# Hybrid encoder layer on one core: down stage begun during the last channel tile, its seven products reordered, its last product in groups of twelve, and two mixer orders changed

## The chip, the cores and the metric

The kernel runs on one core of a Trainium2 chip. The metric is the device time of one execution in microseconds (us), from three runs; the median is compared. A profile of one execution gives the trace that is read here.

The engines by the names of the trace: PE is the matrix engine (PEld its weight loads), DVE the vector engine, ACT the scalar engine, POOL the general engine, SP the engine that issues most transfers. Each works through its own instructions in order and waits on the others through semaphores. PEclk is the clock that was granted to PE, 1.00 being full speed.

## The reference, cut to what matters

One layer over 1280 tokens: 256 of a prompt (tiles t = 0, 1 of 128 tokens) and 1024 of a sample (t = 2 to 9), with shared weights, width 1024, feed-forward width 2816 = 22 tiles of 128 channels.

```python
h  = rmsnorm(x, g_pre_mix) * (1 + scale1) + shift1
y  = mixer(h)            # gated spatial mixing || gated linear attention, then @ w_out
x  = x + gate1 * rmsnorm(y, g_post_mix)
h  = rmsnorm(x, g_pre_ffn) * (1 + scale2) + shift2
up = conv(h @ w_up) + b_conv          # width-3 convolution along the tokens
gate, val = split(up)
y  = (silu(gate) * val) @ w_down      # 1280 x 2816 @ 2816 x 1024
x  = x + gate2 * rmsnorm(y, g_post_ffn)
```

Everything is fp32 to the outside. Inside, an fp32 operand is split into a rounded part `hi` and a rest `lo`, and a product is three matmuls: hi·hi, hi·lo, lo·hi.

## The kernel before, in words

**Stages.** Modulation vectors; in-projection; the mixer (spatial gating beside gated linear attention); `mix_out` (product with `w_out`, norm, residual); the up stage, first over the prompt (f = 0 to 21), then over the sample (f = 0 to 21); the down stage. PE's order is written out by hand; from the mixer on the other engines' instructions are put in order by a scheduler, from their dependences and estimated costs.

**Mixer.** For each pair of heads and chunk, `s3` adds into one PSUM bank: for each half j one full-height matmul `scT` (128x128) and two half-height matmuls against the state `St` (output 64 rows). There are 20 such steps, each among matmuls of the in-projection.

**mix_out.** Tile t loads the old x into the one buffer `xb` (L932, on SP's queue), squares y on ACT (L936), scales and adds it on DVE (L942, L944).

**Up stage of the sample.** A channel tile f is 7 products of 12 matmuls (84 at L1155) into three PSUM banks X, Y, V by a Strassen-Winograd scheme. `ug` and `uv` are taken out by ACT and DVE (L1162 to L1174), two convolutions follow (L1041, L1045), Silu (L1178), the product `av` on DVE (L1180), and a store of `av` to memory `g_d[f]`, 512 KB, on SP's queue (L1073). That store is kept in `gst` and issued a tile later, the last one behind the loop.

**Down stage.** `g` (tokens in two halves r, `half_tiles`) times `w_down` (columns in two halves n) is seven Strassen products, each 11 k-steps of two channel tiles (k = 0 to 10) x 5 token tiles j x 3 matmuls = 165 matmuls of 128x512 (L1300), in the order M3, M5, M2, M4, M1, M7, M6. Operand A is `g` (A00 of half r = 0 and even channel tiles, and so on; 320 KB each), B is `w_down` (256 KB each). For each k, `ops_of` loads what isn't resident (SP's queue), adds or subtracts on DVE where the product wants a sum (L1240, `saM`, `sbM`), and splits: hi on ACT (L91), lo on DVE (L92), into `aoM` (ring of 4) and `boM` (ring of 5). A00, A11 and B11 for k < 7 stay resident. Within a product PE runs k = 0, 1 together, then k = 2 to 8 one by one, and the last two k-steps (three in M6) j by j, so that a token tile ends early and `evac` adds its bank into the result y (L1280; or ACT where it is set). When a piece of y has had its last product, `finish` squares it on ACT (L1252) and multiplies it in place by the gate row G2 on DVE (L1253); when both halves of a row are done, `emit` loads x, makes the factor rf on POOL (L1261, L1262), and adds on DVE (L1265) and stores each half. M7 ends the five tiles of half 0, M6 those of half 1. The PSUM banks of the down stage are a pool of eight, opened when the up stage's pools are closed; G2 (1 MB) is loaded on ACT's queue.

Of the kernel before, what the change touches and what calls it, by code (L numbers as in the profile page):

```python
# [34 lines left out]
def encoder_kernel(ctx: ExitStack, tc: tile.TileContext, x_prompt, x_sample, c_prompt, c_sample,  # L35
# [693 lines left out]
    def s3(h, i):  # L729
# [9 lines left out]
        for j in range(2):  # L739
            nc.tensor.matmul(op[:, j, :], scT[n % RING][:, j, :], v[:, j, :], start=True, stop=False,  # L740
                             skip_group_check=True)
# [455 lines left out]
    nc.scalar.dma_start(Gbc2.rearrange("p s c -> p (s c)"), gate_d[1].to_broadcast([P, 2 * D]))
    ares, bres = {}, {}

    def load_a(r, c, k):  # L1200
        if r == c:
            if (r, k) not in ares:
                t = ares[(r, k)] = dr.tile([P, 640], F32, name=f"A{r}{c}_{k}")
                nc.sync.dma_start(t, g_d[2 * k + c][r])
# [4 lines left out]

    def load_b(c, n, k):  # L1210
        if c and n and k in bres:
            return bres[k]
# [5 lines left out]
        nc.sync.dma_start(raw, w_down[P * f:P * f + P, 512 * n:512 * n + 512])
# [9 lines left out]
    y = {}  # L1228
    ssq = {t: dn.tile([P, 2], F32, name=f"fssq{t}") for t in range(NT)}
    done = set()  # L1230

    def ops_of(i, k):
        name, a, b, _ = prods[i]
        src = []
        for what, terms, load, n, tag in ((0, a, load_a, 640, "sa"), (1, b, load_b, 512, "sb")):
            t0 = load(*terms[0], k)
            if len(terms) > 1:
                t1 = load(*terms[1], k)
                s = dr.tile([P, n], F32, tag=tag, name=f"{tag}{name}_{k}", bufs=2)
                nc.vector.tensor_tensor(out=s, in0=t0, in1=t1, op=ALU.add if terms[2] > 0 else ALU.subtract)  # L1240
# [16 lines left out]
    def emit(t, n):
# [5 lines left out]
        for n in range(2):  # L1263
            cs_ = slice(512 * n, 512 * n + 512)
            nc.vector.scalar_tensor_tensor(out=xo[:, cs_], in0=y[t][:, cs_], scalar=r, in1=xo[:, cs_],  # L1265
                                           op0=ALU.mult, op1=ALU.add)
# [24 lines left out]
    for i in range(len(prods)):  # L1291
        last = i == len(prods) - 1
        pss = [dp.tile([P, 512], F32, tag="d", name=f"dn{i}_{j}") for j in range(5)]
        ops = {}

        def mmk(j, k):
            ao, w = ops[k]
            cs_ = slice(P * j, P * j + P)
            for q, (ai, wi) in enumerate(((0, 0), (0, 1), (1, 0))):
                nc.tensor.matmul(pss[j], ao[:, ai, cs_], w[:, wi, :], start=(k == 0 and q == 0),  # L1300
                                 stop=(k == NK - 1 and q == 2))
# [51 lines left out]
```

## Time and profile before

| what | value |
|---|---|
| runs | 1463.11, 1468.05, 1467.68 us, median 1467.68 us |
| profiled execution | 1463.15 us, its span 1461.4 us |
| mean granted PE clock | 0.980 |
| PE busy | 1385.5 us, 95% of the span |
| DVE, ACT, POOL busy | 75%, 47%, 39% |
| down stage, 1155 matmuls | from 1177.58 us, last bank complete at about 1449.4 us |
| transfers | mean 144 GB/s; 277 and 307 GB/s in the two slices of about 37 us that follow 1169 us |

In the timeline a row is: start us, duration us, engine, line, operation, out<-in, shapes, count, and in brackets the idle time of that engine before it with what ended it. "SPq" and "ACTq" are transfers at the moment at which they are issued. In the windows a row gives the busy time and number of instructions of each engine in that stretch, then the granted PE clock, the share of the transfer engines and GB/s.

### The profile page before, as it was taken

The numbers are of one execution on the slowest core, as the hardware profiler recorded it, in microseconds if no ns is written. First come the engines' busy times: TensorE is split into PE (matmuls) and PEld (weight loads), VectorE is DVE, ScalarE is ACT, GpSimd is POOL, SyncE is SP. The second block draws the span as 40 slices with busy tenths as digits, with TensorE's granted clock in tenths as the row PEclk, the third lists the DMA queues.
The fourth block names the chain that finished last, engine by engine and source line by source line (L and its number), as shares of the span: only waits on it lengthen the run. The fifth ranks groups of instructions, "written<-read, shape, count | busy, mean of one in ns | idle before, by whom it ended". The sixth has DMA issues, their size and how long they took to land.

```text
span 1461.4 us, 20550 instructions
## 1 busy us (share of the span) xinstructions
PE 1385.5 (95%) x7057; PEld 1131.6 (77%) x7057; DVE 1089.4 (75%) x1653; ACT 692.5 (47%) x1405; POOL 576.3 (39%) x663
## 2 busy tenths in 40 slices
PE   8999989899997999898999999999999989999986
PEld 5886667677776888897978888888888868888875
DVE  5677667877744456798768888788778677879997
ACT  4544465645333234456654555545544345544342
POOL 3356756778763011443454444444444200001011
PEclk9999999999999999999999999999999999999998
DMA  9568542332223442565642222222222288551586
GB/s 300 195 226 289 189 124 84 117 97 63 84 91 110 145 152 101 154 175 156 196 131 85 87 76 66 83 87 87 87 87 80 81 277 307 181 169 65 186 287 207
DMA packets 204107, 210.53 MB, mean 144 GB/s; under 512 B 12968, under 2 KB 157668, under 8 KB 201700
## 3 DMA queue, kind: packets, MB, share of 16 engines
q1 hardware_dynamic: 199976, 200.10, 43.0%
q10 hardware_dynamic: 4028, 9.14, 1.6%
q8 instruction: 55, 0.90, 0.3%
q14 instruction: 48, 0.39, 0.1%
HBM read 171.16 MB, written 38.03 MB: 143 GB/s over the span
## 4 chain that ended last, share of the span: by engine, by line
PE 66%; DVE 10%; issue 7%; DMA 6%; POOL 6%; ACT 4%; SPq 0%; DVEq 0%; POOLq 0%; ACTq 0%
PE upX L1155 16%; PE dn L1300 15%; PE upV L1155 8%; PE ps_gb L338 5%; PE ps_ga L338 4%; PE upY L1155 4%; DMA raw_p<-in_w_up_dram 3%; PE y L878 3%; PE y L879 3%; PE y L881 2%; DVE St L723 1%; POOL macc L466 1%; DVE accP L1041 1%; POOL rstd L98 1%; PE ds L704 1%
## 5 line engine op out<-in xcount | busy, mean ns | idle before, releaser
L1300 PE MATMUL dn<-boM,aoM 128*128 128x512 f32 x1155 | 266.6, 393 | 11.1 <-ACT boM L91 5.9
L1300 PEld LDWEIGHTS dn<-boM,aoM 128*128 128x128 f32 x1155 | 219.4, 190 | 58.2 <-ACT boM L91 6.3
L92 POOL TENSOR_TENSOR ws_S<-S,ws_S 128x512 fp32r<-128x512 f32 x66 | 110.5, 1676 | 102.8 <-ACT ws_S L91 102.8
L1093 PE MATMUL upP<-hp,wp 128*128 128x256 f32 x1056 | 133.7, 287 | 14.4 <-DVE wp L92 12.9
L1093 PEld LDWEIGHTS upP<-hp,wp 128*128 128x128 f32 x1056 | 130.2, 192 | 17.6 <-DVE wp L92 15.4
L1155 PE MATMUL upX<-bop_T,ws_S 128*128 128x512 f32 x528 | 130.0, 395 | 2.8 <-ACT ug L1162 2.8
L92 POOL TENSOR_TENSOR ws<-raw_s,ws 128x512 fp32r<-128x512 f32 x44 | 77.2, 1756 | 120.6 <-ACT ws L91 120.6
L1155 PEld LDWEIGHTS upX<-bop_T,ws_S 128*128 128x128 f32 x528 | 100.0, 189 | 25.8 <-ACT ug L1162 3.3
L338 PE MATMUL ps_ga<-w_a,h1hi 128*128 128x512 f32 x320 | 105.6, 408 | 3.3 <-POOL w_a L92 2.6
L338 PE MATMUL ps_gb<-w_b,h1hi 128*128 128x512 f32 x320 | 105.9, 411 | 1.0 <-DVE w_b L92 0.5
L91 ACT ACTIVATE ws_S<-S 128x512 fp32r<-128x512 f32 x88 | 55.0, 628 | 85.6 <-DVE S L1135 53.8
L92 POOL TENSOR_TENSOR wp<-raw_p,wp 128x512 fp32r<-128x512 f32 x44 | 62.5, 1421 | 75.9 <-ACT wp L91 75.5
L1255 POOL TENSOR_SCALAR fssq<-fssq 128x1 f32<-128x1 f32 x10 | 9.7, 967 | 181.1 <-ACT junk L1252 181.1
L338 PEld LDWEIGHTS ps_ga<-w_a,h1hi 128*128 128x128 f32 x320 | 59.3, 190 | 22.5 <-issue 4.2
L91 ACT ACTIVATE aoM<-saM 128x640 fp32r<-128x640 f32 x55 | 40.6, 740 | 71.7 <-DVE saM L1240 27.4
L1135 DVE TENSOR_TENSOR S<-raw_s,raw_s 128x512 f32<-128x512 f32 x44 | 72.1, 1640 | 3.2 <-DMA raw_s<-in_w_up_dram 3.2
L338 PEld LDWEIGHTS ps_gb<-w_b,h1hi 128*128 128x128 f32 x320 | 57.8, 191 | 14.7 <-issue 2.4
L1041 DVE SCALAR_TENSOR_TENSOR ag<-ug,c,ag 128x1023 f32<-128x1023 f32 x44 | 56.5, 1284 | 15.9 <-ACT ag L1045 15.2
L91 ACT ACTIVATE wp<-raw_p 128x512 fp32r<-128x512 f32 x88 | 53.7, 627 | 30.8 <-DMA raw_p<-in_w_up_dram 25.4
L98 POOL TENSOR_TENSOR rstd<-ms,mhalf 128x2 f32<-128x2 f32 (+1 forms) x90 | 65.3, 726 | 7.3
L338 PE MATMUL ps_gb<-w_b,h1lo 128*128 128x512 f32 x160 | 65.3, 408 | 0.0
L338 PE MATMUL ps_ga<-w_a,h1lo 128*128 128x512 f32 x160 | 65.3, 408 | 0.0
(269 smaller groups left out, 3256.0 us busy)
## 6 DMA issues: line engine op xcount, KB each, us to landing
raw_d<-in_w_down_dram SPq DMA_DIRECT2D x104, 256.0 KB
raw_p<-in_w_up_dram SPq DMA_DIRECT2D x88, 256.0 KB
raw_s<-in_w_up_dram SPq DMA_DIRECT2D x88, 256.0 KB
A<-g_d SPq DMA_DIRECT2D x66, 320.0 KB
wa<-in_w_ada_dram SPq DMA_DIRECT2D x16, 1024.0 KB
g_d<-av SPq DMA_DIRECT2D x22, 512.0 KB
wa<-in_w_ada_dram SPq DMA_DIRECT2D x16, 512.0 KB
vr_d<-vr SPq DMA_DIRECT2D x20, 256.0 KB
```

What stands on the lines that cost most here:

```text
L91: nc.scalar.activation(w[:, 0, :], raw, AF.Copy)
L92: (eng or nc.gpsimd).tensor_tensor(out=w[:, 1, :], in0=raw, in1=w[:, 0, :].bitcast(F32), op=ALU.subtract)
L98: nc.gpsimd.tensor_tensor(out=r, in0=ms, in1=mhalf.to_broadcast([P, n]) if n > 1 else mhalf, op=ALU.pow)
L338: nc.tensor.matmul(ps, st, mv, start=(i == 0), stop=(i == n - 1))
L878: nc.tensor.matmul(ys[n], mh[:, kt, :], wos[(kt, n)][:, 0, :], start=(i == 0), stop=False)
L879: nc.tensor.matmul(ys[n], mh[:, kt, :], wos[(kt, n)][:, 1, :], start=False, stop=False)
L881: nc.tensor.matmul(ys[n], ml[:, kt, :], wos[(kt, n)][:, 0, :], start=False, stop=(i == KT - 1))
L1041: nc.vector.scalar_tensor_tensor(out=acc[:, o:o + b - a], in0=src[:, a:b], scalar=c2[:, i, fi:fi + 1], in1=acc[:, o:o + b - a], op0=ALU.mu ...
L1093: nc.tensor.matmul(ps[:, half, :], st, hp[:, hi, kt, :], start=(kt == 0 and i == 0 and half == 0), stop=(kt == KT - 1 and i == 2), skip_gr ...
L1135: nc.vector.tensor_tensor(out=s, in0=a, in1=b, op=op)
L1155: nc.tensor.matmul(ps, w[:, wi, P * j:P * j + P], bops[(b, j)][:, hi, :], start=(start and j == 0 and i == 0), stop=(stop and j == 3 and i ...
L1300: nc.tensor.matmul(pss[j], ao[:, ai, cs_], w[:, wi, :], start=(k == 0 and q == 0), stop=(k == NK - 1 and q == 2))
```

## The change

1. **Down stage begun earlier.** In f = 21 the operands of M3 for k = 0, 1 go into a pool of their own, `er`: A00 (`ea_k`) and the two weight tiles (`raw_e`) are loaded at the head of the last channel tile, their difference is made in place, and they are split (`eao`, `ebo`). The 30 matmuls of k = 0, 1 stand directly behind the last matmul of the up stage. To have banks for it, the down stage takes its PSUM tiles from the up stage's two pools (`bank`) and opens none. Since A00_0, A00_1, B11_0 and B11_1 did not become resident in M3, M5 loads them.
2. **Buffers given out in a set order** (`new_as`, `firsts` and the loops behind it), so that the addresses of these tiles follow the order of these calls.
3. **Order of products** M3, M5, M1, M7, M4, M2, M6: M4 now ends the tiles of half 0, and in M4 the piece (1, 0) is set, in M2 added to.
4. **`finish` writes into a tile of its own** (`yg`, ring of 2) for the second half of a row.
5. **Tail of four k-steps** in M6: twelve matmuls for each j in place of nine.
6. **`s3`**: both scT matmuls first, then the four St matmuls; the bank is started once.
7. **`mix_out`**: `xb` is loaded on ACT's queue.

```diff
-            nc.tensor.matmul(op[:, j, :], scT[n % RING][:, j, :], v[:, j, :], start=True, stop=False,
+            nc.tensor.matmul(op[:, j, :], scT[n % RING][:, j, :], v[:, j, :], start=(j == 0), stop=False,
                              skip_group_check=True)
+        for j in range(2):
             for e in range(2):
...
-        xloads[t] = nc.sync.dma_start(xt, x_rows(t))
+        xloads[t] = nc.scalar.dma_start(xt, x_rows(t))
...
+    def early_load():
+        for k in range(2):
+            a = er.tile([P, 640], F32, name=f"ea_{k}")
+            nc.sync.dma_start(a, g_d[2 * k][0])
+            b = [raw_tile(f"raw_e{k}_{c}") for c in range(2)]
+            for c in range(2):
+                nc.sync.dma_start(b[c], w_down[P * (2 * k + c):P * (2 * k + c) + P, 512:1024])
+            eops.append((a, b))
+
+    def early_split():
+        for k, (a, b) in enumerate(eops):
+            nc.vector.tensor_tensor(out=b[0], in0=b[0], in1=b[1], op=ALU.subtract)
+            ao = er.tile([P, 2, 640], F32R, name=f"eao_{k}")
+            bo_ = er.tile([P, 2, 512], F32R, name=f"ebo_{k}")
+            split(ao, a, nc.vector)
+            split(bo_, b[0], nc.vector)
+            eops[k] = [[t[:, h, :] for h in range(2)] for t in (ao, bo_)]
+
+    def bank(name):
+        i = banks["i"] % 8
+        banks["i"] += 1
+        return gpa.tile([P, 512], F32, tag="g", name=name) if i in (3, 4) else fp.tile([P, 512], F32, tag="f", name=name)
...
+        if f == NFF - 1:
+            er, er_close = pool("er", side="right")
+            early_load()
         while gst:
             gst.pop(0)()
...
         nc.scalar.activation(uv[:, lo], X, AF.Copy)
+        if f == NFF - 1:
+            early_split()
+            pss0 = [bank(f"dn0_{j}") for j in range(5)]
+            for k in range(2):
+                for j in range(5):
+                    mmk(pss0[j], *eops[k], j, k)
...
     gst.pop(0)()
     sf_close()
     hb_close()
+    er_close()
...
-    dp, dp_close = pool("dp", bufs=8, space=PSUM)
...
+    firsts = [new_as("A_first"), new_sum("sa", 640, "sa_first")]
+    for k in range(2):
+        new_ar(1, k)
+    firsts += [new_sum("sb", 512, "sb_first"), new_ao("ao_first"), new_bo("bo_first")]
+    for k in range(2, NK):
+        new_ar(1, k)
...
-             ("M2", ((1, 0), (1, 1), 1), ((0, 0),), ((1, 0, "set"), (1, 1, "sub"))),
-             ("M4", ((1, 1),), ((1, 0), (0, 0), -1), ((0, 0, "add"), (1, 0, "add"))),
              ("M1", ((0, 0), (1, 1), 1), ((0, 0), (1, 1), 1), ((0, 0, "add"), (1, 1, "add"))),
              ("M7", ((0, 1), (1, 1), -1), ((1, 0), (1, 1), 1), ((0, 0, "add"),)),
+             ("M4", ((1, 1),), ((1, 0), (0, 0), -1), ((0, 0, "add"), (1, 0, "set"))),
+             ("M2", ((1, 0), (1, 1), 1), ((0, 0),), ((1, 0, "add"), (1, 1, "sub"))),
              ("M6", ((1, 0), (0, 0), -1), ((0, 0), (0, 1), 1), ((1, 1, "add"),)))
...
-        nc.vector.tensor_tensor(out=y[t][:, cs_], in0=y[t][:, cs_], in1=Gbc2[:, 0 if t < 2 else 1, cs_], op=ALU.mult)
+        yg = y[t][:, cs_] if (t, 1 - n) not in done else dn.tile([P, 512], F32, tag="yg", name=f"yg{t}", bufs=2)
+        ygs[(t, n)] = yg
+        nc.vector.tensor_tensor(out=yg, in0=y[t][:, cs_], in1=Gbc2[:, 0 if t < 2 else 1, cs_], op=ALU.mult)
...
-        pss = [dp.tile([P, 512], F32, tag="d", name=f"dn{i}_{j}") for j in range(5)]
+        pss = [bank(f"dn{i}_{j}") for j in range(5)] if i else pss0
...
-        tail = 3 if last else 2
-        for k in range(NK - tail):
+        tail = 4 if last else 2
+        for k in range(0 if i else 2, NK - tail):
```

The order of the transfers that SP issues where the two stages meet, before (`raw_d01_k` and `B11_k` are the weight tiles of M3, `A00_k` its operand A, `g_d20` and `g_d21` the stores of the last two channel tiles):

```order
L1073 DMA g_d20_85<-av20_10947 128x2x512
L1204 DMA A00_0_11134<-g_d0_65 128x640
L1218 DMA B11_0_11138<-in_w_down_dram 128x512
L1204 DMA A00_1_11148<-g_d2_67 128x640
L1218 DMA B11_1_11152<-in_w_down_dram 128x512
L1204 DMA A00_2_11192<-g_d4_69 128x640
L1218 DMA B11_2_11196<-in_w_down_dram 128x512
L1204 DMA A00_3_11221<-g_d6_71 128x640
L1073 DMA g_d21_86<-av21_11091 128x2x512
L1218 DMA B11_3_11225<-in_w_down_dram 128x512
```

And now:

```order
L1279 DMA raw_d01_2_11224<-in_w_down_dram 128x512
L1279 DMA raw_d01_3_11251<-in_w_down_dram 128x512
L1279 DMA raw_d01_4_11278<-in_w_down_dram 128x512
L1279 DMA raw_d01_5_11305<-in_w_down_dram 128x512
L1074 DMA g_d20_85<-av20_10947 128x2x512
L1074 DMA g_d21_86<-av21_11155 128x2x512
L1264 DMA A00_2_11211<-g_d4_69 128x640
L1279 DMA B11_2_11212<-in_w_down_dram 128x512
L1264 DMA A00_3_11209<-g_d6_71 128x640
L1279 DMA B11_3_11210<-in_w_down_dram 128x512
```

The loads of A00 and B11 for k = 2 and A00 for k = 3 stood ahead of the last store; now they stand behind it, and four weight tiles stand ahead of both stores.

DVE where the up stage ends, before (`av21` is the last product of the up stage, `sbM3_k` the difference of two weight tiles of M3 for k, `aoM3_k` and `boM3_k` the lo parts):

```order
L1041 SCALAR_TENSOR_TENSOR av21_11091<-uv21_10998,c2_5056,av21_11091 128x1023 x2
L1240 TENSOR_TENSOR sbM3_0_11140<-raw_d01_0_11136,B11_0_11138 128x512
L1180 TENSOR_TENSOR av21_11091<-ag21_11090,av21_11091 128x1024
L92 TENSOR_TENSOR aoM3_0_11142<-A00_0_11134,aoM3_0_11142 128x640
L92 TENSOR_TENSOR boM3_0_11145<-sbM3_0_11140,boM3_0_11145 128x512
L1240 TENSOR_TENSOR sbM3_1_11154<-raw_d01_1_11150,B11_1_11152 128x512
```

And now:

```order
L1042 SCALAR_TENSOR_TENSOR av21_11155<-uv21_11013,c2_5056,av21_11155 128x1023 x2
L1224 TENSOR_TENSOR av21_11155<-ag21_11154,av21_11155 128x1024
L1301 TENSOR_TENSOR sbM3_2_11227<-raw_d01_2_11224,B11_2_11212 128x512
L1301 TENSOR_TENSOR sbM3_3_11254<-raw_d01_3_11251,B11_3_11210 128x512
L92 TENSOR_TENSOR aoM3_2_11229<-A00_2_11211,aoM3_2_11229 128x640
L92 TENSOR_TENSOR boM3_2_11232<-sbM3_2_11227,boM3_2_11232 128x512
```

The first work of DVE for the down stage at this place is that of k = 2, and the difference for k = 3 stands ahead of both lo parts of k = 2.

DVE in the tail of M6, before:

```order
L1280 TENSOR_TENSOR y1_11431<-dn6_0_13174,y1_11431 128x512
L1253 TENSOR_TENSOR y1_11431<-y1_11431,G2_11117 128x512
L1265 SCALAR_TENSOR_TENSOR xo1_13488<-y1_11431,rf1_13490,xo1_13488 128x512 x2
L1280 TENSOR_TENSOR y6_11441<-dn6_1_13175,y6_11441 128x512
L1280 TENSOR_TENSOR y7_11451<-dn6_2_13176,y7_11451 128x512
L1253 TENSOR_TENSOR y6_11441<-y6_11441,G2_11117 128x512
L1265 SCALAR_TENSOR_TENSOR xo6_13510<-y6_11441,rf6_13512,xo6_13510 128x512 x2
```

And now:

```order
L1343 TENSOR_TENSOR y1_11448<-dn6_0_13189,y1_11448 128x512
L1316 TENSOR_TENSOR yg1_13490<-y1_11448,G2_11177 128x512
L1328 SCALAR_TENSOR_TENSOR xo1_13492<-y1_11448,rf1_13494,xo1_13492 128x512
L1328 SCALAR_TENSOR_TENSOR xo1_13492<-yg1_13490,rf1_13494,xo1_13492 128x512
L1343 TENSOR_TENSOR y6_11458<-dn6_1_13190,y6_11458 128x512
L1316 TENSOR_TENSOR yg6_13516<-y6_11458,G2_11177 128x512
L1328 SCALAR_TENSOR_TENSOR xo6_13518<-y6_11458,rf6_13520,xo6_13518 128x512
```

Before, the additions of the second and third tile stood together, and of the fourth and fifth; now each tile's additions, product and sums stand together before the next tile's begin.

More of the change, by code (lines that the diff above doesn't have):

```diff
@@ L1116, in encoder_kernel, with mmk @@
     sf, sf_close = pool("sf")
+    NK = NFF // 2
+    er = None
+    eops = []
+    def early_load():
[14 more added lines that the diff above has]
+            eops[k] = [[t[:, h, :] for h in range(2)] for t in (ao, bo_)]
+    banks = {"i": 0}
+    def bank(name):
+        i = banks["i"] % 8
+        banks["i"] += 1
+        return gpa.tile([P, 512], F32, tag="g", name=name) if i in (3, 4) else fp.tile([P, 512], F32, tag="f", name=name)
+    def mmk(ps, ao, w, j, k):
+        cs_ = slice(P * j, P * j + P)
+        for q, (ai, wi) in enumerate(((0, 0), (0, 1), (1, 0))):
+            nc.tensor.matmul(ps, ao[ai][:, cs_], w[wi], start=(k == 0 and q == 0), stop=(k == NK - 1 and q == 2))
     for f in range(NFF):
@@ L1198, in encoder_kernel @@
     ares, bres = {}, {}
+    new_as = lambda name: dr.tile([P, 640], F32, tag="as", name=name, bufs=4)
+    new_sum = lambda tag, n, name: dr.tile([P, n], F32, tag=tag, name=name, bufs=2)
+    new_ao = lambda name: dr.tile([P, 2, 640], F32R, tag="ao", name=name, bufs=4)
+    new_bo = lambda name: dr.tile([P, 2, 512], F32R, tag="bo", name=name, bufs=5)
+    new_ar = lambda r, k: ares.setdefault((r, k), dr.tile([P, 640], F32, name=f"A{r}{r}_{k}"))
+    new_br = lambda k: bres.setdefault(k, dr.tile([P, 512], F32, name=f"B11_{k}"))
+    firsts = [new_as("A_first"), new_sum("sa", 640, "sa_first")]
[4 more added lines that the diff above has]
+        new_ar(1, k)
+    for k in (1, 0):
+        new_ar(0, k), new_br(k)
+    for k in range(NK - 1, 1, -1):
+        new_ar(0, k)
+        if k < 7:
+            new_br(k)
+    loaded = set()
     def load_a(r, c, k):
         if r == c:
-            if (r, k) not in ares:
-                t = ares[(r, k)] = dr.tile([P, 640], F32, name=f"A{r}{c}_{k}")
-                nc.sync.dma_start(t, g_d[2 * k + c][r])
+            if (r, k) not in loaded:
+                loaded.add((r, k))
+                nc.sync.dma_start(ares[(r, k)], g_d[2 * k + c][r])
             return ares[(r, k)]
-        t = dr.tile([P, 640], F32, tag="as", name=f"A{r}{c}_{k}", bufs=4)
+        t = new_as(f"A{r}{c}_{k}")
         nc.sync.dma_start(t, g_d[2 * k + c][r])
@@ L1210, in load_b @@
     def load_b(c, n, k):
-        if c and n and k in bres:
+        if c and n and ("b", k) in loaded:
             return bres[k]
@@ L1214, in load_b @@
         if c and n and k < 7:
-            raw = bres[k] = dr.tile([P, 512], F32, name=f"B11_{k}")
+            raw = bres[k]
+            loaded.add(("b", k))
         else:
@@ L1222, in encoder_kernel @@
              ("M5", ((0, 0), (0, 1), 1), ((1, 1),), ((0, 1, "add"), (0, 0, "neg"))),
[L1223 to L1224 removed]
              ("M1", ((0, 0), (1, 1), 1), ((0, 0), (1, 1), 1), ((0, 0, "add"), (1, 1, "add"))),
              ("M7", ((0, 1), (1, 1), -1), ((1, 0), (1, 1), 1), ((0, 0, "add"),)),
+             ("M4", ((1, 1),), ((1, 0), (0, 0), -1), ((0, 0, "add"), (1, 0, "set"))),
+             ("M2", ((1, 0), (1, 1), 1), ((0, 0),), ((1, 0, "add"), (1, 1, "sub"))),
              ("M6", ((1, 0), (0, 0), -1), ((0, 0), (0, 1), 1), ((1, 1, "add"),)))
[L1228 removed]
+    y, ygs = {}, {}
     ssq = {t: dn.tile([P, 2], F32, name=f"fssq{t}") for t in range(NT)}
@@ L1238, in ops_of @@
                 t1 = load(*terms[1], k)
-                s = dr.tile([P, n], F32, tag=tag, name=f"{tag}{name}_{k}", bufs=2)
+                s = new_sum(tag, n, f"{tag}{name}_{k}")
                 nc.vector.tensor_tensor(out=s, in0=t0, in1=t1, op=ALU.add if terms[2] > 0 else ALU.subtract)
@@ L1242, in ops_of @@
             src.append(t0)
-        ao = dr.tile([P, 2, 640], F32R, tag="ao", name=f"ao{name}_{k}", bufs=4)
+        ao = new_ao(f"ao{name}_{k}")
         split(ao, src[0], nc.vector)
-        wo_ = dr.tile([P, 2, 512], F32R, tag="bo", name=f"bo{name}_{k}", bufs=5)
+        wo_ = new_bo(f"bo{name}_{k}")
         split(wo_, src[1], nc.vector)
-        return ao, wo_
+        return [[t[:, h, :] for h in range(2)] for t in (ao, wo_)]
     def finish(t, n):
@@ L1264, in emit @@
             cs_ = slice(512 * n, 512 * n + 512)
-            nc.vector.scalar_tensor_tensor(out=xo[:, cs_], in0=y[t][:, cs_], scalar=r, in1=xo[:, cs_],
+            nc.vector.scalar_tensor_tensor(out=xo[:, cs_], in0=ygs[(t, n)], scalar=r, in1=xo[:, cs_],
                                            op0=ALU.mult, op1=ALU.add)
@@ L1292, in encoder_kernel @@
         last = i == len(prods) - 1
-        pss = [dp.tile([P, 512], F32, tag="d", name=f"dn{i}_{j}") for j in range(5)]
+        pss = [bank(f"dn{i}_{j}") for j in range(5)] if i else pss0
         ops = {}
[L1296 to L1301, printed above, removed]
-        tail = 3 if last else 2
-        for k in range(NK - tail):
+        tail = 4 if last else 2
+        for k in range(0 if i else 2, NK - tail):
             ops[k] = ops_of(i, k)
-            if k == 0:
+            if i and k == 0:
                 continue
-            if k == 1:
+            if i and k == 1:
                 for js in ((0, 1, 2), (3, 4)):
@@ L1311, in encoder_kernel @@
                         for j in js:
-                            mmk(j, kk)
+                            mmk(pss[j], *ops[kk], j, kk)
                 continue
             for j in range(5):
-                mmk(j, k)
+                mmk(pss[j], *ops[k], j, k)
         for k in range(NK - tail, NK):
@@ L1319, in encoder_kernel @@
             for k in range(NK - tail, NK):
-                mmk(j, k)
+                mmk(pss[j], *ops[k], j, k)
             evac(i, j, pss[j])
-    for close in (dp_close, dn_close, dr_close, rp_close, cp_close, dram_close):
+    for close in (fp_close, gpa_close, dn_close, dr_close, rp_close, cp_close, dram_close):
         close()
```

3 lines of the change are left out of this document (removed).

## The prediction

> **What bounds the kernel now.** I read the page first (who is busy, the chain that ended last), then PE's waits, then the places of these waits in the timeline, and there the granted clock.
>
> ```profile
> PE 1385.5 (95%) x7057; PEld 1131.6 (77%) x7057; DVE 1089.4 (75%) x1653; ACT 692.5 (47%) x1405; POOL 576.3 (39%) x663
> ...
> GB/s 300 195 226 289 189 124 84 117 97 63 84 91 110 145 152 101 154 175 156 196 131 85 87 76 66 83 87 87 87 87 80 81 277 307 181 169 65 186 287 207
> ...
> PE 66%; DVE 10%; issue 7%; DMA 6%; POOL 6%; ACT 4%; SPq 0%; DVEq 0%; POOLq 0%; ACTq 0%
> ```
>
> PE is the bound. The change removes no matmul, so it can only win at PE's waits, at matmuls that run on a lower clock, and in the tail behind PE's last matmul. PE's waits of the stages that are touched:
>
> ```profile
> PE pt_m L781 <- DMA m<-m_d: 7.3, 1, 7.3
> PE dn L1300 <- ACT boM L91: 5.9, 1, 5.9
> ...
> PE dn L1300 <- DVE aoM L92: 4.2, 1, 4.2
> ```
>
> The first is at the head of the product with w_out, the second where the up stage meets the down stage (the join), the third inside M6. The timeline at the join:
>
> ```profile
> 1166.11 2.88 PE L1155 MATMUL upV<-bop,ws_S 128*128 128x512 f32 x12
> ...
> 1168.83 2.88 PE L1155 MATMUL upX<-bop_T,ws 128*128 128x512 f32 x12
> ...
> 1173.73 1.06 ACT L1178 ACTIVATE ag<-ag 128x1024 f32<-128x1024 f32 x1
> ...
> 1176.78 1.22 DVE L1180 TENSOR_TENSOR av<-ag,av 128x1024 f32<-128x1024 f32 x1
> ...
> 1177.58 0.79 PE L1300 MATMUL dn<-boM,aoM 128*128 128x512 f32 x1 [5.86 <-ACT boM L91]
> ...
> 1178.02 0.37 SPq L1073 DMA_DIRECT2D g_d<-av  x1
> 1178.44 0.47 SPq L1218 DMA_DIRECT2D B<-in_w_down_dram  x1
> ...
> 1178.65 0.69 DVE L92 TENSOR_TENSOR boM<-sbM,boM 128x512 fp32r<-128x512 f32 x1
> ...
> 1179.39 10.79 PE L1300 MATMUL dn<-boM,aoM 128*128 128x512 f32 x40 [1.02 <-DVE boM L92]
> ...
> 1179.85 0.82 DVE L92 TENSOR_TENSOR aoM<-A,aoM 128x640 fp32r<-128x640 f32 x1
> ...
> 1179.97 0.33 ACTq L1197 DMA_DIRECT2D G<-gate_d  x1
> 1180.32 0.43 SPq L1218 DMA_DIRECT2D B<-in_w_down_dram  x1
> ...
> 1180.85 0.38 SPq L1204 DMA_DIRECT2D A<-g_d  x1
> ...
> 1188.56 0.69 DVE L1240 TENSOR_TENSOR sbM<-raw_d,B 128x512 f32<-128x512 f32 x1 [3.36 <-DMA B<-in_w_down_dram]
> ...
> 1189.80 0.74 ACT L91 ACTIVATE aoM<-A 128x640 fp32r<-128x640 f32 x1 [2.65 <-DMA A<-g_d]
> ```
>
> Twelve matmuls at full clock start 1168.83 - 1166.11 = 2.72 us apart, 0.2267 each; the last of the up stage ends at 1177.58 - 5.86 = 1171.72. The last product of the up stage on DVE ends at 1178.0, and only then does SP issue its store. Later loads take long here: the weight tile for k = 4, issued at 1180.32, is used 8.24 us later after a wait for it, the A tile issued at 1180.85 after 8.95 us. The clock and the transfers in windows of 1 us, at the join and at M6:
>
> ```profile
> 1175.00:1176.00 1.00, 0.00 (x0) 0.00 (x0) 1.00 (x1) 1.00 (x2) 0.00 (x0) 0.85 0.00 0
> ...
> 1181.00:1182.00 1.00, 1.00 (x4) 0.81 (x3) 1.00 (x3) 0.27 (x2) 0.00 (x0) 0.50 0.99 306
> 1182.00:1183.00 1.00, 1.00 (x5) 0.73 (x5) 1.00 (x2) 0.59 (x1) 0.00 (x0) 0.74 0.86 252
> ...
> 1414.00:1415.00 1.00, 0.00 (x0) 0.00 (x0) 0.72 (x2) 0.00 (x0) 0.00 (x0) 0.81 0.70 262
> ...
> 1421.00:1422.00 1.00, 1.00 (x5) 0.81 (x4) 1.00 (x2) 0.42 (x1) 0.00 (x0) 0.77 0.91 308
> ```
>
> 0.85 in one window means that the clock halved at 1175.70, 4.0 us after PE stopped; 0.74 that it was whole again at 1182.5. At M6 it halved at 1414.6 and was whole at 1421.5. Matmuls lose half of the time in between. Full transfer engines move about 306 GB/s. The stall in M6:
>
> ```profile
> 1401.24 0.68 DVE L1280 TENSOR_TENSOR y<-dn,y 128x512 f32<-128x512 f32 x1
> ...
> 1404.19 1.42 DVE L1265 SCALAR_TENSOR_TENSOR xo<-y,rf,xo 128x512 f32<-128x512 f32 x2 [0.46 <-POOL rf L1262]
> ...
> 1410.37 1.42 DVE L1265 SCALAR_TENSOR_TENSOR xo<-y,rf,xo 128x512 f32<-128x512 f32 x2 [0.44 <-POOL rf L1262]
> ...
> 1414.60 1.42 DVE L1265 SCALAR_TENSOR_TENSOR xo<-y,rf,xo 128x512 f32<-128x512 f32 x2 [0.28 <-DMA xo<-x_d]
> 1415.93 0.82 DVE L92 TENSOR_TENSOR aoM<-saM,aoM 128x640 fp32r<-128x640 f32 x1
> ...
> 1416.80 3.78 PE L1300 MATMUL dn<-boM,aoM 128*128 128x512 f32 x8 [4.23 <-DVE aoM L92]
> ```
>
> From 1401.24 to 1415.93 DVE does nothing but end the five tiles of half 0, and the lo part that PE needs for k = 2 stands behind that. The stall costs 4.23 us and half of 1416.80 to 1421.5, 2.3 us.
>
> **The change part by part.** The sum starts from the profiled execution, 1463.15 us (span 1461.4), which is 4.5 us under the median of the runs.
>
> Join. Before, PE lost 5.86 + 1.02 us in waits, and between 1177.58 and 1182.5 it worked 3.9 us at half clock, which is 2.0: 8.9 in all. Now the 30 matmuls of k = 0, 1 follow the up stage directly, 30 x 0.2267 = 6.8 us, and end at 1178.5. That part I take as done: their sums and splits stand in f = 20 and before, where DVE and ACT aren't what PE waits for, at most one difference of DVE, 0.69 us, late, and this moves nothing if k = 2 decides. But k = 2 now decides. Its loads (A00 and B11) stand on SP behind the last store, which waits for DVE until 1178.0. So they are issued from about 1178.4, one each 0.43 us: A00_2, B11_2, A00_3, B11_3 at about 1179.8. DVE takes the difference for k = 3 ahead of the lo parts of k = 2, so B11_3 counts too. Store and four loads are 512 + 640 + 512 KB = 1.70 MB; from 1178.9 at 306 GB/s that is 5.6 us, 1184.5. G2's 1 MB is now issued right behind Silu (ends at 1174.8), near 1175.5, into idle transfer engines (0.00 above), and I take it as out of the way. Then 0.69 + 0.82 + 0.69 on DVE (the rows of 1188.56, 1179.85, 1178.65): k = 2 starts at 1186.7. PE's idle time is 8.2 us, with some 2.0 at half clock behind it (1.6 to 2.3): 10.2, so the join is +1.3. Low end: the four loads alone, 3.8 us from 1178.5, k = 2 at 1184.6, -1.1. High end: B11_3 lands 8.95 us after its issue, at 1188.8, k = 2 at 1191.0, 12.5 + 2.3, +6.0. What the edit takes from PE's wait for k = 0, 1 it gives back at k = 2.
>
> Order of products. M4 now does what M7 did, and M2 waits where M6 did: five additions, five products with G2 and ten sums stand between M4's last matmul and the lo part of k = 2. Two things are lighter: M4 and M2 need one sum for each k and not two, so DVE isn't late at the start of the burst (0.7 us or so: M7's first tile was complete 24 + 30 matmuls, 12.2 us, before the stall of 1412.6, at about 1400.4), and `yg` lets the product go ahead without ACT, with other work in front of the sums, which can save up to the 0.46 + 0.44 + 0.28 us of waits. That leaves 2.3 to 4.2; I take 2.7, -1.5. The clock fell 2.0 us after PE stopped in M6, 4.0 us at the join; a stall of 2.7 lies between, so I take half of the 2.3 us away: -1.2. Doubt about the burst itself takes 0.7 back: -2. Ends: all of it gone, -6.5; nothing gained and M4 half a microsecond worse, +0.5.
>
> [...]
>
> The tail:
>
> ```profile
> 1437.66 11.72 PE L1300 MATMUL dn<-boM,aoM 128*128 128x512 f32 x51
> ...
> 1441.26 0.69 DVE L1280 TENSOR_TENSOR y<-dn,y 128x512 f32<-128x512 f32 x1 [2.19 <-PE dn L1300]
> ...
> 1444.15 1.41 DVE L1265 SCALAR_TENSOR_TENSOR xo<-y,rf,xo 128x512 f32<-128x512 f32 x2 [0.72 <-POOL rf L1262]
> ...
> 1445.48 1.28 DVE L1280 TENSOR_TENSOR y<-dn,y 128x512 f32<-128x512 f32 x2
> ...
> 1456.55 1.41 DVE L1265 SCALAR_TENSOR_TENSOR xo<-y,rf,xo 128x512 f32<-128x512 f32 x2
> ```
>
> PE ends at T = 1449.38, DVE at 1457.96, T + 8.6. One tile alone takes 1445.48 - 1441.26 = 4.22 us on DVE, most of it waiting for ACT and POOL; before, tiles two to five went in pairs, 6.2 us each. Now the first tile is complete four groups of 12 before T, T - 10.9 (before T - 8.2), but DVE does the tiles one after the other: -10.9 + 0.2 + 5 x 4.22 = T + 10.4, +1.8 us. Ends: -2.4, if ACT and POOL are quicker than in that row since the product no longer waits; +2.5. With four k-steps in the tail all four `aoM` tiles are in use, and the last can be split only when k = 6 is through: ACT 0.74, DVE 0.82 + 0.69 against nine matmuls, 2.0 us: +0.2.
>
> The mixer. Where a half-height matmul is followed by a full one, the weight load stands 0.17 us without cause:
>
> ```profile
> 268.20 0.30 PEld L740 LDWEIGHTS o<-v,scT 128*128 128x128 f32 x2 [0.17 <-issue]
> ...
>   issue: 3.4, 20
> ```
>
> One of two such places goes in each of 20 steps, 3.4 us at most; some groups wait for other engines later and swallow it: -2 (-3.4 to 0).
>
> `xb` on ACT's queue. Ten issues move from SP to ACT. SP gains nothing where PE waits. The first one now stands ahead of the load behind PE's 7.3 us wait:
>
> ```profile
> 471.35 0.38 SPq L773 DMA_DIRECT2D m<-m_d  x1
> ```
>
> 512 KB at 306 GB/s are 1.7 us, if all of it is in the way: +0.5 (0 to +1.7).
>
> M5's four reloads are 1.15 MB. They lie beside 37 us of matmuls; the transfers of this time (307 and 181 GB/s in the page's slices from 1205 and 1242) also hold what is fetched ahead, so 0; without that cover 1.15 MB / 306 GB/s = 3.8 us.
>
> Sum: +1.3 - 2 + 1.8 + 0.2 - 2 + 0.5 = -0.2, so 1463.0 on the profiled execution's level and 1467.5 on the median's. The runs lie at both, so I say 1465.
>
> **The rivals.** Faster, by M2: the burst on DVE fits beside PE's 30 matmuls of k = 0, 1, so the whole stall and its half clock go (-6.5); with the lighter loads at the join (-1.1) and all of the mixer's 3.4, against +2.5 in tail and transfers, -8.5: 1456.5. For it: the waits of 1.2 us within the burst and the late start of 0.7. Against it: these make 1.9, and the stall is 4.2.
>
> Faster, by the join: the loads of k = 2 aren't late after all, and the 8.9 us go but for 1 or so: 1465 - 9 = 1456. Against it stands SP's order.
>
> Slower, by the join: everything that is issued between 1175.5 and 1182 shares the transfer engines: store, G2 and eight loads, 512 + 1024 + 2304 KB = 3.93 MB, 12.8 us at 306 GB/s from 1178.9. B11_3 then lands at 1191.7, k = 2 starts at 1193.9: PE loses 15.4 + 2.3, +8.8 in place of +1.3: 1472.5. For it: the tiles that took 8.24 and 8.95 us. Against it: G2 was issued among those, at 1179.97, and comes earlier now. It decides (over 0.5% against the median) once k = 2 starts after 1194.
>
> [...]
>
> **How the numbers follow.** 0.5%, about 7.3 us, is what a measurement of this kernel can tell from no change. Forecast (terms cancel) 0.57, M2 free 0.25, join free 0.07, join late 0.11. The two faster rivals end near that bound, so some of them is "same", as some of the forecast's lower part is "faster": faster 0.31, same 0.59, slower 0.10. The range reaches to the rivals on both sides: the forecast alone gives 1458 to 1470, with them 1454 to 1473.
>
> **What would show it.** Join: down matmuls directly behind the up stage, then one wait of about 8 us at x30, with DVE waiting for a B tile; a wait under 3 us proves me wrong there. M2: a wait of 2 to 4 us for aoM at k = 2, with or without half clock; none at M6. Tail: DVE ends 10 us behind PE, not 8.6. Mixer: L740's idle time of 3.4 us at issue about gone, the in-projection's end some 2 us earlier. pt_m's wait within 1.7 us of 7.3. The forecast is wrong if a new wait shows in M5 or M1, or if k = 2 at the join starts before 1183 or after 1194.

## The result, and the profile after

The changed kernel takes 1475.19 us (median of 11 runs), the kernel before 1467.68 us in the same comparison: ratio 1.0057, 95% interval 1.0043 to 1.0071. It is slower by some 8 us, more than the range allowed for (1473) and on the side to which I had given one chance in ten.

The profiled execution has a span of 1471.1 us (before 1461.4). Its page and PE's waits, the rows that answer to those of before and the new ones:

```profile
PE 1384.1 (94%) x7057; PEld 1132.8 (77%) x7057; DVE 1094.0 (74%) x1653; ACT 690.6 (47%) x1405; POOL 571.9 (39%) x663
```

```profile
PE pt_m L782 <- DMA m<-m_d: 7.1, 1, 7.1
PE dn L1150 <- ACT boM L91: 6.5, 2, 5.9
...
PE upX L1193 <- ACT ug L1200: 4.9, 3, 1.8
PE dn L1150 <- DVE aoM L92: 4.3, 1, 4.3
...
PE upV L1193 <- ACT uv L1206: 1.8, 1, 1.8
```

Two kinds of rows are new: PE waits for ACT's `ug` three times (before once), and for `uv`; both are in the up stage of the sample, whose work the change doesn't touch. The first, in the timeline where f = 1 ends and in f = 2:

```profile
781.27 0.34 SPq L1125 DMA_DIRECT2D ea<-g_d  x1
...
784.21 0.74 ACT L91 ACTIVATE eao<-ea 128x640 fp32r<-128x640 f32 x1 [3.27 <-DMA ea<-g_d]
...
792.29 0.58 ACT L1200 ACTIVATE ug<-upX 128x512 f32<-128x512 f32 x1
...
792.93 3.01 PE L1193 MATMUL upX<-bop_T,ws_S 128*128 128x512 f32 x12 [1.51 <-ACT ug L1200]
```

The early operand A for k = 0 is split on ACT at the end of f = 1, 390 us before it is needed. ACT stands 3.27 us before it for the load, which SP had issued only just before, and everything behind it on ACT is late: `ug` of f = 2, and with it PE. The same happens two tiles on for k = 1 (PE waits 1.59 us in f = 4). The second kind, in f = 20:

```profile
1148.88 2.34 SPq L1128 DMA_DIRECT2D raw_e<-in_w_down_dram  x2
1150.17 0.69 DVE L1133 TENSOR_TENSOR raw_e<-raw_e,raw_e 128x512 f32<-128x512 f32 x1 [1.36 <-DMA raw_e<-in_w_down_dram]
1150.89 0.63 ACT L91 ACTIVATE ebo<-raw_e 128x512 fp32r<-128x512 f32 x1 [4.92 <-DVE raw_e L1133]
1151.43 0.58 ACT L1206 ACTIVATE uv<-upV 128x512 f32<-128x512 f32 x1
...
1152.06 3.06 PE L1193 MATMUL upV<-bop,ws_S 128*128 128x512 f32 x12 [1.80 <-ACT uv L1206]
```

ACT waits 4.92 us for DVE's difference, DVE waits for the weight tiles, and V's evacuation stands behind; PE had gone on to the next product at 1147.4, so that it was held up for some 3.3 us of this. The first products of f = 20 and f = 21 in the changed kernel, and in the kernel before:

```profile
1136.33 2.97 PE L1193 MATMUL upX<-bop,ws 128*128 128x512 f32 x12
...
1158.26 2.89 PE L1193 MATMUL upX<-bop,ws 128*128 128x512 f32 x12
```

```profile
1133.16 2.97 PE L1155 MATMUL upX<-bop,ws 128*128 128x512 f32 x12
...
1152.37 2.88 PE L1155 MATMUL upX<-bop,ws 128*128 128x512 f32 x12
```

21.93 us in place of 19.21: f = 20 is 2.7 us longer.

The join:

```profile
1177.44 6.96 PE L1150 MATMUL dn<-ebo,eao 128*128 128x512 f32 x30
...
1179.63 0.33 ACTq L1238 DMA_DIRECT2D G<-gate_d  x1
1182.26 1.23 DVE L1224 TENSOR_TENSOR av<-ag,av 128x1024 f32<-128x1024 f32 x1
1183.98 0.42 SPq L1264 DMA_DIRECT2D A<-g_d  x1
...
1188.94 0.69 DVE L1301 TENSOR_TENSOR sbM<-raw_d,B 128x512 f32<-128x512 f32 x1 [5.46 <-DMA B<-in_w_down_dram]
...
1190.35 0.79 PE L1150 MATMUL dn<-boM,aoM 128*128 128x512 f32 x1 [5.95 <-ACT boM L91]
...
1193.03 12.34 PE L1150 MATMUL dn<-boM,aoM 128*128 128x512 f32 x42 [1.89 <-DVE boM L92]
```

The 30 matmuls run without a gap behind the up stage, as meant. Then PE waits 5.95 + 1.89 us for k = 2: its first load is issued at 1183.98, behind the last store, and DVE waits for the B tile until 1188.94. The clock in windows of 1 us:

```profile
1188.00:1189.00 1.00, 0.00 (x0) 0.00 (x0) 0.06 (x1) 0.74 (x1) 0.00 (x0) 0.62 0.98 313
...
1198.00:1199.00 1.00, 1.00 (x5) 0.82 (x4) 0.90 (x2) 0.00 (x0) 0.00 (x0) 0.76 0.84 203
```

It halved at 1188.2 and was whole again at 1198.5, with 6.2 us of matmuls at half speed in between: 7.8 + 3.1 = 10.9 us lost, before 8.9. G2 is not what the loads waited for: in the windows from 1180 to 1184 the transfer engines moved 139, 352, 377 and 172 GB/s, 1.04 MB, about as much as G2 has, so that it was through when the store was issued, at 1183.51.

The stall of M6 is now in M2, and M6 has small new ones (PE's rows of the timeline that follow a wait):

```profile
1387.35 58.52 PE L1150 MATMUL dn<-boM,aoM 128*128 128x512 f32 x245 [4.27 <-DVE aoM L92]
1446.40 0.73 PE L1150 MATMUL dn<-boM,aoM 128*128 128x512 f32 x2 [0.54 <-DVE boM L92]
1447.67 0.51 PE L1150 MATMUL dn<-boM,aoM 128*128 128x512 f32 x1 [0.53 <-ACT boM L91]
```

The clock at the stall of M2, in windows of 1 us:

```profile
1386.00:1387.00 1.00, 0.00 (x0) 0.00 (x0) 1.00 (x2) 0.00 (x0) 0.00 (x0) 0.60 0.33 127
...
1393.00:1394.00 1.00, 1.00 (x6) 0.77 (x5) 1.00 (x2) 0.58 (x2) 0.00 (x0) 0.98 0.98 364
```

It was half from 1386.2 to 1393.0, so that PE worked at half speed for 5.7 us behind the stall.

The tail, one token tile from addition to addition and the last sum:

```profile
1452.97 0.69 DVE L1343 TENSOR_TENSOR y<-dn,y 128x512 f32<-128x512 f32 x1
...
1454.55 0.19 POOL L1324 TENSOR_TENSOR rf<-fssq 128x1 f32<-128x1 f32 x1 [2.95 <-ACT junk L1313]
...
1456.74 0.69 DVE L1343 TENSOR_TENSOR y<-dn,y 128x512 f32<-128x512 f32 x1
...
1467.37 0.75 DVE L1328 SCALAR_TENSOR_TENSOR xo<-yg,rf,xo 128x512 f32<-128x512 f32 x1
```

A tile takes 3.77 us and not 4.22. The difference is POOL's addition, 0.2 us against 0.7 in the first tile of before:

```profile
1442.74 0.69 DVE L1253 TENSOR_TENSOR y<-y,G 128x512 f32<-128x512 f32 x1 [0.79 <-ACT junk L1252]
1442.79 0.70 POOL L1261 TENSOR_TENSOR rf<-fssq 128x1 f32<-128x1 f32 x1 [30.00 <-ACT junk L1252]
```

Before, the product with G2 waited for ACT, so that it ran beside POOL's addition, which ended 0.06 us behind it. Now the product goes ahead while ACT squares (1453.69 to 1454.38) and is through when POOL starts. In the bursts and tails of these two traces, all seven of these additions that began beside a product with G2 or a sum into `xo` ended 0.04 to 0.06 us behind it; three that began beside an addition out of PSUM took 0.2. That DVE holds POOL back is what these rows suggest; no run tried it by itself. DVE ends 8.1 us behind PE's last matmul (1460.06), before 8.6.

### The profile page after: what moved, and what is told of

It reads as the page before. It is cut to its first block, busy times and chain, and to the rows that moved or that the text cites. A ratio compares the mean times of both kernels' runs of the same rounds, so it can differ in the third digit from the quotient of the medians.

```text
span 1471.1 us, 20541 instructions
## 1 busy us (share of the span) xinstructions
PE 1384.1 (94%) x7057; PEld 1132.8 (77%) x7057; DVE 1094.0 (74%) x1653; ACT 690.6 (47%) x1405; POOL 571.9 (39%) x663
## 4 chain that ended last, share of the span: by engine, by line
PE 55%; DVE 18%; POOL 7%; DMA 7%; issue 6%; ACT 6%; SPq 0%; POOLq 0%; ACTq 0%; DVEq 0%
PE dn L1150 14%; PE upX L1193 14%; PE upV L1193 7%; PE upY L1193 3%; PE y L879 3%; PE y L880 3%; PE y L882 3%; PE ps_gb L338 2%; PE ps_ga L338 2%; DVE accP L1042 2%; DVE St L723 2%; POOL rstd L98 1%; DMA raw_p<-in_w_up_dram 1%; PE ps_qkS L347 1%; POOL gg L640 1%
## 5 line engine op out<-in xcount | busy, mean ns | idle before, releaser
L1150 PE MATMUL dn<-boM,aoM 128*128 128x512 f32 x1125 | 262.3, 396 | 13.4 <-ACT boM L91 6.5
L1150 PEld LDWEIGHTS dn<-boM,aoM 128*128 128x128 f32 x1125 | 214.9, 191 | 60.8 <-ACT boM L91 7.3
L1193 PE MATMUL upV<-bop,ws_S 128*128 128x512 f32 x264 | 64.3, 393 | 1.9 <-ACT uv L1206 1.8
L879 PE MATMUL y<-wo,mh 128*128 128x512 f32 x160 | 65.1, 407 | 0.0
```

Of the source, the lines that this page charges most:

```text
L879: nc.tensor.matmul(ys[n], mh[:, kt, :], wos[(kt, n)][:, 0, :], start=(i == 0), stop=False)
L1150: nc.tensor.matmul(ps, ao[ai][:, cs_], w[wi], start=(k == 0 and q == 0), stop=(k == NK - 1 and q == 2))
L1193: nc.tensor.matmul(ps, w[:, wi, P * j:P * j + P], bops[(b, j)][:, hi, :], start=(start and j == 0 and i == 0), stop=(stop and j == 3 and i ...
```

## The experiments

Each was timed against the kernel before, in turns on the same chip; kernels of different rounds are compared through their ratios. Ratios are to the kernel before, with 95% intervals; 0.1% is 1.5 us.

| kernel | ratio | interval |
|---|---|---|
| the changed kernel | 1.0057 | 1.0043 to 1.0071 |
| early_only | 1.0069 | 1.0053 to 1.0086 |
| rest_only | 1.0011 | 0.9992 to 1.0029 |
| mixer_only | 0.9997 | 0.9982 to 1.0012 |
| order_only | 0.9992 | 0.9975 to 1.0009 |
| yg_tail | 1.0018 | 1.0001 to 1.0036 |
| ea_late | 1.0035 | 1.0020 to 1.0051 |
| splits_late | 1.0023 | 1.0003 to 1.0042 |
| store_act | 0.9989 | 0.9969 to 1.0010 |
| three_fixes | 0.9966 | 0.9950 to 0.9982 |
| three_oldtail | 0.9955 | 0.9937 to 0.9974 |
| early_fixed | 0.9942 | 0.9922 to 0.9961 |

**Which part costs.** `early_only` is the changed kernel with the other five edits undone:

```diff
-             ("M1", ...), ("M7", ...), ("M4", ...), ("M2", ...),
+             ("M2", ...), ("M4", ...), ("M1", ...), ("M7", ...),
-        yg = y[t][:, cs_] if (t, 1 - n) not in done else dn.tile(...)
+        yg = y[t][:, cs_]
-        tail = 4 if last else 2
+        tail = 3 if last else 2
```

and s3 and xb as before. `rest_only` is the kernel before with those five edits, without the early start.

> Only the early start (with its buffers and banks) is made; products, tail, finish and mixer as before. My theory now: the early start loses by itself, in two places: in f = 20 PE waits for V's bank, since ACT's split of the early weights stands ahead of its evacuation (2.7 us), and the join loses some 2 us more than before, since the loads of k = 2 stand behind the last store. So +3 to +6 us against the kernel before, with a PE wait of about 1.8 us in f = 20 and two of about 6 and 2 us at the join. Rival (the other edits are what costs, the early start is even): within 1 us of before.

> All edits but the early start. My theory: about even, -1 to +2 us: the mixer gains 1 to 2, the M2 stall costs as much as the M6 stall did, k = 7 to 10 of M6 wait 1.3 us for the ring of four aoM, the tail behind PE is about 1 us shorter. Rival (the other edits are what costs): +4 us or more.

The early start alone is slower by 10.1 us (7.8 to 12.6), all others together by 1.6 (-1.2 to +4.3). PE's waits of early_only show the same places as the changed kernel:

```profile
800.18 3.02 PE L1192 MATMUL upX<-bop_T,ws_S 128*128 128x512 f32 x12 [1.36 <-ACT ug L1199]
840.43 3.02 PE L1192 MATMUL upX<-bop_T,ws_S 128*128 128x512 f32 x12 [1.45 <-ACT ug L1199]
1159.09 3.03 PE L1192 MATMUL upV<-bop,ws_S 128*128 128x512 f32 x12 [1.73 <-ACT uv L1205]
1197.97 0.79 PE L1149 MATMUL dn<-boM,aoM 128*128 128x512 f32 x1 [6.73 <-ACT boM L91]
1200.12 226.27 PE L1149 MATMUL dn<-boM,aoM 128*128 128x512 f32 x991 [1.36 <-DVE boM L92]
```

My expectation, +3 to +6, missed the first two of these waits; I found them only in this run. With them this trace accounts for 2.8 us in f = 2 and 4, 2.5 in f = 20 and 1.0 at the join (8.1 us of waits and 1.8 of half clock, before 8.9 in all): 6.3 us, less than the lower end of the interval. The rest isn't placed. The first product of f = 0 starts 7.0 us later than in the trace of before (749.3 against 742.3), but in this place the traces of all thirteen kernels spread between these two, whatever the edits.

**The two mixer edits.** The kernel before with these two edits (and `start=(j == 0)` in the first, as in the change):

```diff
+        for j in range(2):
             for e in range(2):
...
-        xloads[t] = nc.sync.dma_start(xt, x_rows(t))
+        xloads[t] = nc.scalar.dma_start(xt, x_rows(t))
```

> Only the order in s3 and xb on ACT's queue. My theory: -2 to 0 us, L740's idle time at issue (3.4 us) gone. Rival (transfers on ACT's queue or the new order delay other engines in the mixer and mix_out): +1 to +3 us, with more waits of PE between 230 and 600 us than before.

No change that can be measured. L740's idle time at issue, 3.4 us before, is gone (no such row in this run's answer or the changed kernel's), but little of it reaches the stage's end. From the first `scT` matmul of the 20 steps to the last `St` matmul it is 188.4 us before and 187.1 here; in the five traces with the old order 187.9 to 189.9, in the eight with the new one 187.0 to 188.5, on average 1.4 us less, too little for the times to show. Matmuls of the next state update wait longer for DVE, 6.4 us where the kernel before had 5.0 (L704, same view):

```profile
PE ds L704 <- DVE klp L692: 6.4, 6, 3.6
```

In the traces with the old order this wait is 4.8 to 6.0 us, with the new one 5.6 to 6.6, so that it took a part of the gain is likely; by itself it isn't shown. The wait for `m`, 7.3 us before, is 7.1 in the changed kernel: it didn't grow with xb's load ahead of it.

**The order of the products, alone:**

```diff
-             ("M2", ...), ("M4", ...),
              ("M1", ...), ("M7", ...),
+             ("M4", ..., ((0, 0, "add"), (1, 0, "set"))),
+             ("M2", ..., ((1, 0, "add"), (1, 1, "sub"))),
```

> Only the order of the seven products is changed, with what is set and added. My theory: M4 now ends the tiles of half 0 and the stall of 4.2 us moves from M6 to M2 with its half clock, so within 1.5 us of before. Rival (the prediction: less work of DVE around the stall): 2 us or more faster, with a stall under 3 us.

Even. The stall is there, 35 us earlier and hardly smaller:

```profile
1382.35 70.61 PE L1300 MATMUL dn<-boM,aoM 128*128 128x512 f32 x298 [3.88 <-DVE aoM L92]
```

The lighter loads of M4 and M2 on DVE gave at most 0.35 us of the 1.5 that I had put down for them, and not even that is shown: with the old order the stall is between 3.86 (early_fixed) and 4.9 us (mixer_only). Its half clock lasts 6.8 us, as before (the 298 matmuls take some 3 us more than at 0.2267 each).

**The product with G2 in a tile of its own, and the tail of four k-steps**, in the kernel before:

```diff
+        yg = y[t][:, cs_] if (t, 1 - n) not in done else dn.tile([P, 512], F32, tag="yg", name=f"yg{t}", bufs=2)
...
-        tail = 3 if last else 2
+        tail = 4 if last else 2
```

> The kernel before with only the product with G2 into a tile of its own and the tail of four k-steps. My theory: PE waits about 1.3 us for k = 8 to 10 of M6, DVE ends some 8.0 us behind PE and not 8.6: 0 to +1.5 us. Rival (the prediction): DVE ends 10.4 us behind PE, +2 us.

2.6 us slower (0.1 to 5.3). PE waits in M6:

```profile
1443.24 0.50 PE L1302 MATMUL dn<-boM,aoM 128*128 128x512 f32 x1 [1.37 <-ACT boM L91]
1444.18 11.63 PE L1302 MATMUL dn<-boM,aoM 128*128 128x512 f32 x50 [0.44 <-DVE boM L92]
```

1.8 us here, 1.3 in the changed kernel. It isn't the ring of four `aoM` that holds them up, as the prediction and I had it. Between 1421 us and these waits neither ACT nor DVE waits for PE in either trace; ACT waits for sums of DVE, and DVE works with gaps of 1.0 us in all here and 0.2 in the changed kernel. In the changed kernel ACT makes the hi parts for k = 10 without a wait for PE:

```profile
1445.12 0.74 ACT L91 ACTIVATE aoM<-saM 128x640 fp32r<-128x640 f32 x1
...
1446.98 0.63 ACT L91 ACTIVATE boM<-sbM 128x512 fp32r<-128x512 f32 x1 [1.12 <-DVE sbM L1301]
```

DVE's sums and lo parts for a k take 2.7 us, and the tail of four k-steps asks for all four within the 2.7 us of its first twelve matmuls, so the last one or two come late. DVE ends 8.0 us behind PE. Of the expectation's two numbers the interval fits both; the rows speak for the first.

**The loads behind the last store.** The changed kernel with this store on ACT's queue:

```diff
-            gst.append(lambda: nc.sync.dma_start(g_d[f][:, :, c0:c0 + n]...
+            gst.append(lambda: (nc.scalar if f == NFF - 1 and n == 512 else nc.sync).dma_start(g_d[f][:, :, c0:c0 + n]...
```

> The changed kernel with the last store of the up stage on ACT's queue, so that the loads of k = 2 and later don't stand behind it on SP. My theory: the loads are issued 15 us earlier, PE waits at the join about 2 us and not 7.8, and the clock stays whole: 7 to 9 us less than the changed kernel, about even with the kernel before. Rival (the loads are slow because the transfer engines are full, wherever they are issued): the join's wait stays at 6 us or more and the time within 2 us of the changed kernel, +5 to +8 against before.

10 us faster than the changed kernel and even with the kernel before. The join:

```profile
1189.19 0.50 PE L1150 MATMUL dn<-boM,aoM 128*128 128x512 f32 x1 [1.39 <-ACT boM L91]
1190.13 187.54 PE L1150 MATMUL dn<-boM,aoM 128*128 128x512 f32 x826 [0.44 <-DVE boM L92]
```

1.83 us of waiting in place of 7.84, and the granted clock stays at 1.00 in all windows of the join (the 826 matmuls take 0.227 us each, as before at full clock): 9.1 us of the 10.9 are back. SP issues the first load of k = 2 at 1168.48, 12.4 us before the up stage ends. So what stood in the way was the store's place in SP's order, not the rate of the transfers. The waits of the up stage stay (1.73 us in f = 20).

**The waits of the up stage.** In `splits_late` the two hi parts of operand A and the two differences of the weights, from which all other parts of the early start are made, take a factor from a tile that holds 1.0 and is written in f = 21, so they can't be put earlier; in `ea_late` only those of operand A do.

```diff
+        if f == NFF - 1:
+            gate = er.tile([P, 1], F32, name="gate")
+            nc.gpsimd.tensor_scalar(gate, ug[:, 0:1], 0.0, 1.0, op0=ALU.mult, op1=ALU.add)
...
-            nc.vector.tensor_tensor(out=b[0], in0=b[0], in1=b[1], op=ALU.subtract)
+            nc.vector.scalar_tensor_tensor(out=b[0], in0=b[0], scalar=gate, in1=b[1], op0=ALU.mult, op1=ALU.subtract)
...
-            split(ao, a, nc.vector)
+            nc.scalar.activation(ao[:, 0, :], a, AF.Copy, scale=gate)
+            nc.vector.tensor_tensor(out=ao[:, 1, :], in0=a, in1=ao[:, 0, :].bitcast(F32), op=ALU.subtract)
```

> The changed kernel with the splits of the early operands held back to f = 21 (they take a factor 1.0 from a small tile that is made behind f = 21's first evacuation); the last store stays on SP. My theory: PE's waits for ug in f = 2 and f = 4 (1.5 and 1.6 us) and for uv in f = 20 (1.8, the tile 2.7 us longer) go, the join stays as it is: 5 to 6 us less than the changed kernel, +1 to +3 against before. Rival (these waits are swallowed again at the join, where k = 2 sets the time): within 2 us of the changed kernel.

> The changed kernel with only the splits of the early A operand held back to f = 21; those of the weights stay in f = 20, the store stays on SP. My theory: the waits for ug in f = 2 and f = 4 go (3.1 us), the wait in f = 20 stays: 3 us less than the changed kernel, +3 to +5 against before. Rival (these two waits are noise of the execution, as that of f = 0 is): as the changed kernel.

Both as the theory said: ea_late is 0.22% under the changed kernel (3.2 us), splits_late 0.34% (5.0 us). The interval of ea_late still overlaps with the changed kernel's, that of splits_late just doesn't; but the waits that were meant to go are gone in both traces. In splits_late the up stage has one wait left, that of f = 0, which the kernel before has too, and the join is as long as in the changed kernel:

```profile
755.43 3.04 PE L1194 MATMUL upX<-bop_T,ws_S 128*128 128x512 f32 x12 [0.48 <-ACT ug L1201]
1187.19 0.79 PE L1151 MATMUL dn<-boM,aoM 128*128 128x512 f32 x1 [5.79 <-ACT boM L91]
1190.21 190.12 PE L1151 MATMUL dn<-boM,aoM 128*128 128x512 f32 x826 [2.23 <-DVE boM L92]
```

In ea_late the wait of f = 20 is still there. So a delay in the up stage isn't swallowed at the join: k = 2 hangs on the last store, the store on the up stage's last product, and all of it moves together.

**Both mended.** `three_fixes` joins splits_late and store_act; `three_oldtail` has besides the tail and the product in place as before; `early_fixed` is early_only with both mendings.

> The changed kernel with the splits held back to f = 21 and with the last store on ACT's queue. My theory: both gains add up, -5 to -8 us against before, no wait of PE for ACT's ug or uv beyond that of f = 0, and at the join at most 2 us. Rival (the join then waits for something else, G2 or DVE): no better than store_act, -1 us.

> As three_fixes, but with the tail of three k-steps and the product with G2 in place, as before. My theory: PE's waits for k = 8 to 10 in M6 (1.3 us) go, the tail behind PE is 0.5 to 1 us longer: within 1 us of three_fixes. Rival (the first theory of the prediction, that the serial tail costs 1.8 us): 2 us faster than three_fixes.

> Only the early start, with its splits held back to f = 21 and the last store on ACT's queue; products, tail, finish and mixer as before. My theory: -5 to -8 us against before, as far below it as three_oldtail, since the other edits are about even. Rival (part of three_oldtail's gain is the mixer's or the new order's): -3 us or less.

All three are faster than both kernels. early_fixed, with nothing but the mended early start, is 8.5 us faster than before (5.7 to 11.4, six runs); three_oldtail and three_fixes gain 1.9 and 3.5 us less, and the intervals overlap. The 1.6 us between these two don't decide between the theories on the tail. The rest of the change brings nothing that adds to the early start. PE's waits in early_fixed from the second channel tile on:

```profile
1182.19 0.51 PE L1150 MATMUL dn<-boM,aoM 128*128 128x512 f32 x1 [1.38 <-ACT boM L91]
1183.13 226.55 PE L1150 MATMUL dn<-boM,aoM 128*128 128x512 f32 x991 [0.44 <-DVE boM L92]
1413.54 32.17 PE L1150 MATMUL dn<-boM,aoM 128*128 128x512 f32 x133 [3.86 <-DVE aoM L92]
```

## Why the prediction was wrong

**The step that failed** is the sentence on the early operands: "their sums and splits stand in f = 20 and before, where DVE and ACT aren't what PE waits for, at most one difference of DVE, 0.69 us, late", and "this moves nothing if k = 2 decides". Both halves were wrong. I counted the splits as work (0.6 to 0.8 us each in the rows) on engines with idle time, and so put them at nothing, and did not ask what they wait for: ACT works in order, and each split waits for a transfer, 3.27 us ahead of f = 2 and 4.92 (through DVE) in f = 20, with the evacuations that PE needs queued behind it. That made 1.5 + 1.6 + 2.7 us. And k = 2 doesn't absorb a late up stage, since its loads hang on the last store: splits_late gave back 5.0 us of the 8.

**The join, k = 2 behind the last store** (+1.3, forecast PE idle 8.2 us): right in mechanism and size, measured 7.84 us of idle time and 3.1 at half clock, +2.0 in all. store_act shows the cause. G2 was out of the way, as I had taken it: issued at 1179.63, 2.2 us behind the up stage's last matmul, and through when the store began.

**M2** (-2): mis-sized. Alone it is 0.9992 (0.9975 to 1.0009), and in the changed kernel 4.27 us of stall and 5.7 us at half clock, +0.5. The order of DVE's work in the burst put other waits for POOL (2.3 us in four) in place of those of before (0.9 us in two, and 0.3 for a load).

**The tail** (+1.8, and +0.2 in M6): both mis-sized, in opposite directions. DVE ends 0.5 us sooner behind PE than before, since a tile takes 3.77 us and not the 4.22 of before's first tile, the only one that I could see alone. In M6 the mechanism was wrong as well: PE waits 1.3 us, not 0.2, and not for the ring but for DVE's sums and lo parts.

**The mixer** (-2) and xb (+0.5): the idle gap went as forecast, and about 1.4 us of it show as a shorter stage in the traces; the times can't show so little.

**M5's reloads** (0): no wait of PE shows in M5, so the cover held.

Taken together these parts missed by 5.8 + 0.7 (join) + 2.5 (M2) - 2.3 (tail) + 1.1 (M6) = 7.8 us, and the median lies 7.7 above the 1467.5 of the sum. That they agree so closely is luck, as the traces spread by 7 us ahead of the up stage alone.

The slower rival had the time about right (1472.5) and the wrong cause: the difference for k = 3 waited for its load only until 1190.95, 5.1 us after the issue, not 11.9.

## What to carry to other kernels

Work moved ahead into idle time of an engine that works in order brings its wait for data along (here 3.27 and 4.92 us on ACT): ask of each moved instruction when its operand lands and what is queued behind it, not only how long it takes. Where a stage is begun early, look at the second step's loads too; if they stand in a queue behind the stage's last store, the stall only moves by a step (here 7.84 us of PE at k = 2). An edit that loses may hold a gain: here two small mendings turned +0.7% into -0.6%.
